# Feed-forward of a float32 decoder trunk in two phases, with hi and lo activations streamed as one operand

## Chip, cores, metric

The kernel runs on one NeuronCore of a Trainium2 chip, as one launch. The metric is the device time of the whole program in microseconds (us). Engines are named as in the profile: PE is TensorE (matmul), PEld its weight load, DVE VectorE, ACT ScalarE, POOL GpSimd, SP the queue that issues DMAs.

## What is computed

A trunk of 4 layers on 256 tokens of width 1024, all in float32. Every layer is a macaron: a feed-forward half, a token mixer (differential attention, RWKV-7, sliding-window attention, differential attention), a second feed-forward half. So there are 8 feed-forwards, each with its own weights (34.6 MB).

```python
D_MODEL, SEQ, DEPTH, D_FF = 1024, 256, 4, 2816
def swiglu(h, w_in, w_out):
    gate, up = jnp.split(h @ w_in, 2, axis=-1)
    return (jax.nn.silu(gate) * up) @ w_out
...
    for i in range(DEPTH):
        mod = (cond @ ada_w[i] + ada_b[i])[:, None, :]
        sh1, sc1, g1, sh2, sc2, g2, sh3, sc3, g3 = jnp.split(mod, N_MOD, axis=-1)
        h = modulate(rms_norm(x, norm_g[i, 0]), sh1, sc1)
        x = x + 0.5 * g1 * swiglu(h, ffn_w_in[i, 0], ffn_w_out[i, 0])
        h = modulate(rms_norm(x, norm_g[i, 1]), sh2, sc2)
        ...   # x = x + g2 * mixer(h)
        h = modulate(rms_norm(x, norm_g[i, 2]), sh3, sc3)
        x = x + 0.5 * g3 * swiglu(h, ffn_w_in[i, 1], ffn_w_out[i, 1])
```

## The kernel before

Activations are kept feature-major: a tile is 128 features on the partitions by 256 tokens. A float32 product is carried by float32r (one-pass) matmuls on operands split exactly as x = hi + lo. ACT makes hi (a cast, L266), DVE makes lo (raw minus hi, L268). For one 128x128 block of weights `mm3` (L282) issues three matmuls with 256 columns each: W_hi times a_hi (L284), W_hi times a_lo (L285), W_lo times a_hi (L286). Each has its own weight load, so W_hi is loaded twice. What follows calls such a block a **weight tile**, and one matmul a **pass**.

Weights come in units of 1 MB (128 x 2048 floats) by `load` (L257): SP fetches the unit into one of 4 `raw` buffers, then it is split in chunks of 512 columns into one of 4 `hi` and 4 `lo` buffers. The adaLN modulation vectors are made on DVE from 1 MB `ada` units (L341), spread over the kernel; a feed-forward takes 16 of them.

`ffn` (L596) loops over 11 pairs j of inner tiles (256 inner features). Per j: two units of W_in (gate, up), one unit of W_out of the pair before; 32 weight tiles for gate and up into two PSUM banks (gate of both inner tiles in one, up in the other), then `silu`, product and split of the inner activation `g` (ACT L675 and L678, DVE L676 and L679, each on 128x512), then 16 weight tiles that add the pair's part of the output into four PSUM banks, `acc`, which hold all 8 output tiles for the whole feed-forward. In the last pair `out_last` finishes two output tiles at a time and `residual` (L566) turns each into the new x (DVE L569). For each new x, `stat_add` squares it (ACT L436) and sums the squares (POOL L444, the last ones on PE, L459), and `pre` makes the unscaled split operand `xh` of the next sub-layer (ACT L481, DVE L482).

A sub-layer starts with `first_units` (L511): its first three units run on `xh` while the norm factor is still being computed; `make_h` (L487) then builds the scaled operand `h` (DVE L503 and L506, ACT L505), and `unraw` (L528) scales the banks made from `xh` (DVE L533).

PE, DVE, ACT, POOL and SP each work their own queue in order. A scheduler fixes the order of each queue when the program is built; buffers that are not yet free become waits.

Of the kernel before, what the change touches and what calls it, by code (L numbers as in the profile page):

```python
# [19 lines left out]
P = 128  # L20
# [4 lines left out]
PA, PB = 2, 9  # L25
DFF = 2816
NPAIR = DFF // 256
# [10 lines left out]
# modulation units taken in a feed-forward layer and in the three mixers  # L38
FF_ADA, MIX_ADA = 16, (8, 4, 4)
# [7 lines left out]
# ------------------------------------------------------------------ host layout  # L47
# [90 lines left out]
def _colunits(w):  # L138
    """[1024, n*256] -> [n, 128, 8*256]"""
# [4 lines left out]
def _rowunits(w):  # L144
    """[n*256, 1024] -> [n, 128, 2*1024]"""
# [4 lines left out]
def _layout(i):  # L150
# [33 lines left out]
    w = g["ffn_w_in"].reshape(DEPTH * 2, ND, P, 2, NPAIR, 256)  # L184
    o["ffi"] = np.ascontiguousarray(w.transpose(0, 4, 3, 2, 1, 5).reshape(DEPTH * 2 * NPAIR * 2, P, 2048))
    w = g["ffn_w_out"].reshape(DEPTH * 2 * NPAIR, 2, P, D)
    o["ffo"] = np.ascontiguousarray(w.transpose(0, 2, 1, 3).reshape(DEPTH * 2 * NPAIR, P, 2048))
# [37 lines left out]
# ------------------------------------------------------------------ device  # L225
class Trunk:
    def __init__(self, tc, ctx, aps, plan):
# [7 lines left out]
        self.sl = e(tc.tile_pool(name="sl", bufs=4))  # L235
        self.pp = e(tc.tile_pool(name="pp", bufs=2, space=bass.MemoryType.PSUM))
# [7 lines left out]
    def ps(self, tag):  # L244
        """One PSUM bank; the four tags have two banks each."""
        return self.pp.tile([P, 512], F32, tag="ps" + tag, name=self.n("ps" + tag))

    def slab(self, tag, shape=(P, 2048), dtype=F32):
        return self.sl.tile(list(shape), dtype, tag=tag, name=self.n(tag))

    # -------------------------------------------------- weights
# [5 lines left out]
    def load(self, src, cols=2048, raw=None, pool=False):  # L257
        """DMA a 1 MB unit and split it exactly: returns (hi, lo)."""
# [5 lines left out]
        for o in range(0, cols, self.chunk):  # L264
            sl = slice(o, min(o + self.chunk, cols))
# [5 lines left out]
    def ahead(self, aps, lead=4):  # L271
        """unit(u) -> (hi, lo) of aps[u]; units are loaded up to `lead` ahead of the one asked for."""
        todo, got = list(aps), []

        def unit(u):
            while todo and len(got) < u + lead:
                got.append(self.load(*todo.pop(0)))
            return got[u]

        return unit  # L280

# [6 lines left out]
    # -------------------------------------------------- constants, inputs  # L288
# [1147 lines left out]
```

## Time and profile before

| | |
|---|---|
| median of 3 runs | 2347.99 us (2346.6 to 2350.0) |
| span of the profiled execution (no other time of it is listed) | 2353.5 us |
| PE busy | 2220.3 us, 94% of the span, 17714 matmuls |
| DVE busy | 1752.3 us, 74% |
| ACT busy | 1193.5 us, 51% |
| POOL busy | 371.1 us, 16% |
| HBM read | 501.84 MB |

The page gives busy time by engine over the whole span. A matmul's listed duration contains its pipeline latency, and matmuls overlap; the time that one costs is the distance from its start to the start of the next. The granted clock of PE is listed as a share of full speed: 1.0 is 2.4 GHz, 0.5 is 1.2 GHz. The same caution holds for DVE, whose neighbours overlap by about 0.08 us.

### The profile page before, as it was taken

What the parts mean: (1) busy time and instruction counts of PE and PEld (TensorE: products, weight loads), DVE (VectorE), ACT (ScalarE), POOL (GpSimd) and SP (SyncE); (2) the same over time, 40 slices, a digit from 0 to 9 for tenths busy, and PEclk for the clock granted to TensorE, in tenths of its full rate; (3) what the DMA queues carried; (4) which work ended last, traced back from release to release, by engine and by line L of the source; (5) the groups of instructions that cost most, each with busy time, mean ns of one, the idle gap of its engine ahead of it and who ended that gap; (6) DMA issues with size and microseconds to landing.
All of it is one profiled execution on the core that took longest, in us unless ns stands there. A gap on an engine that the chain in (4) does not pass through costs nothing.

```text
span 2353.5 us, 44720 instructions
## 1 busy us (share of the span) xinstructions
PE 2220.3 (94%) x17714; PEld 2151.1 (91%) x17714; DVE 1752.3 (74%) x3437; ACT 1193.5 (51%) x2594; POOL 371.1 (16%) x1047
## 2 busy tenths in 40 slices
PE   3999889999999899998999999999999999889999
PEld 3999888999999778887999999989999999778999
DVE  6886877988875668876887885668888965777654
ACT  2544656544544455433644644487445544656542
POOL 4000454000100232221100100221001000444000
PEclk9999999999999999988999999999999999999999
DMA  7886454888675410005688695535987765463552
GB/s 284 339 330 223 146 198 179 307 337 322 238 270 191 164 55 19 19 19 182 242 341 314 231 354 180 188 126 185 359 316 285 288 233 180 146 214 126 204 190 73
DMA packets 72498, 505.78 MB, mean 215 GB/s; under 512 B 8032, under 2 KB 10592, under 8 KB 11744
## 3 DMA queue, kind: packets, MB, share of 16 engines
q1 hardware_dynamic: 70992, 501.68, 57.8%
q8 instruction: 139, 2.28, 0.4%
q10 hardware_dynamic: 1296, 1.25, 0.2%
q14 instruction: 71, 0.58, 0.1%
HBM read 501.84 MB, written 1.05 MB: 214 GB/s over the span
## 4 chain that ended last, share of the span: by engine, by line
PE 46%; DVE 8%; POOL 5%; issue 4%; ACT 2%; DMA 0%; DVEq 0%; POOLq 0%; ACTq 0%
PE psa L286 4%; PE psa L285 4%; PE psa L284 4%; PE psd L285 4%; PE psd L286 4%; PE psd L284 3%; PE psb L284 3%; PE psb L285 3%; PE psb L286 3%; PE psc L285 2%; PE psc L284 2%; PE psc L286 2%; DVE lo L268 2%; DVE xh L482 1%; DVE xr L503 1%
## 5 line engine op out<-in xcount | busy, mean ns | idle before, releaser
L266 ACT CAST hi<-raw 128x512 fp32r<-128x512 f32 x1314 | 739.2, 618 | 726.4 <-issue 633.0
L268 DVE TENSOR_TENSOR lo<-raw,hi 128x512 fp32r<-128x512 f32 x1306 | 841.2, 690 | 236.1 <-ACT hi L266 235.1
L284 PE MATMUL psa<-h,hi 128*128 128x256 f32 x1360 | 385.4, 284 | 20.4 <-ACT hi L266 8.1
L285 PE MATMUL psa<-h,hi 128*128 128x256 f32 x1360 | 386.2, 284 | 3.0 <-DVE h L506 3.0
L286 PE MATMUL psa<-h,lo 128*128 128x256 f32 x1360 | 385.6, 284 | 0.0
L285 PE MATMUL psd<-h,hi 128*128 128x256 f32 x1280 | 362.6, 283 | 2.9 <-DVE h L506 2.8
L286 PE MATMUL psd<-h,lo 128*128 128x256 f32 x1280 | 362.1, 283 | 0.5 <-POOL lo L268 0.5
L284 PE MATMUL psd<-h,hi 128*128 128x256 f32 x1280 | 360.7, 282 | 0.0
L341 DVE SCALAR_TENSOR_TENSOR ada<-ada,cb 128x1024 f32<-128x1024 f32 x232 | 276.2, 1224 | 18.3 <-DMA ada<-in_ada_dram 18.2
L284 PEld LDWEIGHTS psa<-h,hi 128*128 128x128 f32 x1360 | 260.9, 192 | 22.0 <-ACT hi L266 8.8
L285 PEld LDWEIGHTS psa<-h,hi 128*128 128x128 f32 x1360 | 259.1, 191 | 4.3 <-DVE h L506 4.1
L286 PEld LDWEIGHTS psa<-h,lo 128*128 128x128 f32 x1360 | 259.1, 191 | 0.0
L285 PEld LDWEIGHTS psd<-h,hi 128*128 128x128 f32 x1280 | 242.7, 190 | 5.3 <-DVE h L506 5.2
L284 PEld LDWEIGHTS psd<-h,hi 128*128 128x128 f32 x1280 | 244.1, 191 | 0.0
L286 PEld LDWEIGHTS psd<-h,lo 128*128 128x128 f32 x1280 | 242.3, 189 | 0.9 <-POOL lo L268 0.8
L286 PE MATMUL psb<-g,lo 128*128 128x256 f32 x704 | 199.3, 283 | 0.0
L284 PE MATMUL psb<-g,hi 128*128 128x256 f32 x704 | 199.3, 283 | 0.0
L285 PE MATMUL psb<-g,hi 128*128 128x256 f32 x704 | 199.2, 283 | 0.0
L285 PE MATMUL psc<-g,hi 128*128 128x256 f32 x704 | 199.0, 283 | 0.0
L286 PE MATMUL psc<-g,lo 128*128 128x256 f32 x704 | 199.0, 283 | 0.0
L284 PE MATMUL psc<-g,hi 128*128 128x256 f32 x704 | 198.9, 283 | 0.0
L484 POOL CAST xh<-shs 128x4 fp32r<-128x4 f32 x80 | 34.7, 441 | 1003.4 <-PE psa L286 528.0
(367 smaller groups left out, 4808.2 us busy)
## 6 DMA issues: line engine op xcount, KB each, us to landing
raw<-in_ffi_dram SPq DMA_DIRECT2D x183, 1024.0 KB, 5.2
ada<-in_ada_dram SPq DMA_DIRECT2D x116, 1024.0 KB, 7.4
raw<-in_ffo_dram SPq DMA_DIRECT2D x88, 1024.0 KB, 5.0
raw<-in_ada_dram SPq DMA_DIRECT2D x24, 1024.0 KB, 4.9
raw<-in_daqk_dram SPq DMA_DIRECT2D x16, 1024.0 KB, 4.9
raw<-in_rwr_dram SPq DMA_DIRECT2D x12, 1024.0 KB, 5.0
raw<-in_dav_dram SPq DMA_DIRECT2D x8, 1024.0 KB, 4.9
raw<-in_dao_dram SPq DMA_DIRECT2D x8, 1024.0 KB, 4.9
```

Source lines behind the costliest of these rows:

```text
L266: nc.scalar.copy(hi[:, sl], raw[:, sl])
L268: eng.tensor_tensor(lo[:, sl], raw[:, sl], hi[:, sl].bitcast(F32), op=ALU.subtract)
L284: nc.tensor.matmul(out, whi, ahi, start=start, stop=False, skip_group_check=True)
L285: nc.tensor.matmul(out, whi, alo, start=False, stop=False, skip_group_check=True)
L286: nc.tensor.matmul(out, wlo, ahi, start=False, stop=stop, skip_group_check=True)
L341: nc.vector.scalar_tensor_tensor(wk, wk, 1.0, self.cond, op0=ALU.mult, op1=ALU.mult, accum_out=raw[:, k:k + 1])
L482: nc.vector.scalar_tensor_tensor(h[:, 1, :T], self.x[d], a[:, d:d + 1], h[:, 0, :T].bitcast(F32), op0=ALU.mult, op1=ALU.subtract)
L484: nc.gpsimd.tensor_copy(h[:, :, T:], self.shs[:, :, d])
L503: nc.vector.scalar_tensor_tensor(t, self.x[d], ac, r, op0=ALU.mult, op1=ALU.mult)
```

## The change

Only `ffn` and the helpers below it change, and two buffer sizes.

- `mm2` takes the place of `mm3` inside the feed-forward, except in the three units that `first_units` runs (two in the very first feed-forward): W_hi times [a_hi | a_lo] as one matmul with 512 columns into the two halves of a PSUM bank, then W_lo times a_hi with 256 columns into the first half. So a weight tile takes two passes and two weight loads in place of three. The sum of the two halves is made when the bank is read: ACT copies the second half to SBUF, DVE adds the first half to it.
- The loop is turned into two phases. Phase 1 goes over 22 single inner tiles f; a unit of W_in now holds gate and up of one inner tile, and each takes a PSUM bank of its own. All 22 `g` tiles stay in SBUF. Phase 2 goes over the 8 output tiles d: 22 weight tiles accumulate in one bank, in two units of 0.72 MB. Then x(d) is formed at once: ACT scales the second half by the gate, POOL (DVE for d of 6 and 7) adds the old x, DVE adds the gated first half; `became` starts `stat_add` and `pre` of it.
- Units are split in chunks of 1024 columns (704 in phase 2); the first four keep 512. `hi` and `lo` have 3 buffers in place of 4. RWKV keeps its r and k in tiles of their own, and no longer in a `hi` and a `lo` buffer.
- The 16 `ada` units of a feed-forward are spread over f = 4 to 19 (10 of them) and d = 0 to 5 (6).

```diff
+    def mm2(self, bank, whi, wlo, a, start, stop):
+        nc.tensor.matmul(bank.rearrange("p (a t) -> p a t", a=2), whi, a, start=start, stop=False,
+                         skip_group_check=True)
+        nc.tensor.matmul(bank[:, :T], wlo, a[:, 0], start=False, stop=stop, skip_group_check=True)
...
-FF_ADA, MIX_ADA = 16, (8, 4, 4)
+FF_ADA, MIX_ADA = (10, 6), (8, 4, 4)
...
+        self.nslab = {"raw": 4, "hi": 3, "lo": 3}
...
+            for f in range(n0, NF):
...
+                w = unit(f)
+                if 4 <= f < 20:
+                    spread(0, 16)
+                tag = "adb"[f % 3]
+                bs = [self.ps(tag), self.ps(tag)]
+                self.project2(w, hs, bs)
+                gt, up = pair()
+                for b, t in zip(bs, (gt, up)):
+                    nc.scalar.copy(t, b[:, T:])
+                    nc.vector.tensor_tensor(t, b[:, :T], t, op=ALU.add)
+                nc.scalar.activation(gt, gt, AF.Silu)
+                finish(gt, up)
...
+            for d in range(ND):
+                bank = self.ps(("aaddbbcb" if rw else "aaddbbcc")[d])
+                for half in range(2):
+                    w = [t[:, :FO].rearrange("p (k c) -> p k c", c=P) for t in unit(NF + 2 * d + half)]
+                    if d < 6:
+                        spread(1, 12)
+                    for k in range(NF // 2):
+                        i = half * (NF // 2) + k
+                        self.mm2(bank, w[0][:, k], w[1][:, k], gs[i], start=(i == 0), stop=(i == NF - 1))
+                t = hp.tile([P, T], F32, tag="gt", bufs=3, name=self.n("hl"))
+                nc.scalar.activation(t, bank[:, T:], AF.Copy, scale=gate[:, d:d + 1])
+                (nc.gpsimd if d < 6 else nc.vector).tensor_tensor(t, t, self.x[d], op=ALU.add)
+                x = self.xp.tile([P, T], F32, tag="x", name=self.n("x"))
+                nc.vector.scalar_tensor_tensor(x, bank[:, :T], gate[:, d:d + 1], t, op0=ALU.mult, op1=ALU.add)
+                self.became(d, x)
...
-                    dst = self.slab(("hi", "lo")[i], (P, ND, T))
+                    dst = rp.tile([P, ND, T], F32, name=self.n("rk"))
```

Inside a feed-forward, PE's queue before, for a gate or up product (psa is the bank, h the activation, hi and lo the weights):

```order
L284 MATMUL psa_7344<-h_7003,hi_7295 128x256
L285 MATMUL psa_7344<-h_7003,hi_7295 128x256
L286 MATMUL psa_7344<-h_7003,lo_7296 128x256
L284 MATMUL psa_7344<-h_7008,hi_7295 128x256
L285 MATMUL psa_7344<-h_7008,hi_7295 128x256
L286 MATMUL psa_7344<-h_7008,lo_7296 128x256
```

and the same place now:

```order
L289 MATMUL psb_4937<-h_4295,hi_4812 128x512
L291 MATMUL psb_4937<-h_4295,lo_4813 128x256
L289 MATMUL psb_4937<-h_4300,hi_4812 128x512
L291 MATMUL psb_4937<-h_4300,lo_4813 128x256
L289 MATMUL psb_4937<-h_4305,hi_4812 128x512
```

Three passes of 256 columns have become one of 512 and one of 256; in all, PE's queue goes from 16148 to 12294 rows.

DVE's queue in the loop over inner tiles, before (gf and g are the product and the lo part of two inner tiles at once, lo the weights' split, the first rows wait for PE):

```order
L676 TENSOR_TENSOR gf_5791<-sil_5790,psa_5793 128x512 [waits PE_49]
L268 TENSOR_TENSOR lo_5969<-raw_5966,hi_5968 128x512 [waits DMAHW1_49,Activation_49]
L268 TENSOR_TENSOR lo_5969<-raw_5966,hi_5968 128x512 [waits Activation_49]
L679 TENSOR_TENSOR g_5789<-gf_5791,g_5789 128x512 [waits Activation_49]
L268 TENSOR_TENSOR lo_5969<-raw_5966,hi_5968 128x512 [waits Activation_49] x2
L341 SCALAR_TENSOR_TENSOR ada_6178,modr_6180<-ada_6178,cb 128x1024 [waits DMAHW5_49]
```

and now, for one inner tile (gt and up are its gate and up parts):

```order
L688 TENSOR_TENSOR gt_5133<-psb_5099,gt_5133 128x256 [waits PE_49]
L352 SCALAR_TENSOR_TENSOR ada_6680,modr_5968<-ada_6680,cb 128x1024 [waits DMAHW1_49]
L352 SCALAR_TENSOR_TENSOR ada_6680,modr_5968<-ada_6680,cb 128x1024
L688 TENSOR_TENSOR up_5134<-psb_5100,up_5134 128x256 [waits Activation_49]
L271 TENSOR_TENSOR lo_5147<-raw_5144,hi_5146 128x1024 [waits DMAHW6_49]
L653 TENSOR_TENSOR up_5134<-gt_5133,up_5134 128x256 [waits DVE_49]
L271 TENSOR_TENSOR lo_5147<-raw_5144,hi_5146 128x1024 [waits Activation_49]
L655 TENSOR_TENSOR g_5140<-up_5134,g_5140 128x256 [waits Activation_49]
```

Four short rows per inner tile (two adds, product, lo part) stand where two long ones per pair stood, and between them the split of a later unit in two rows.

## Rows read from the trace of the kernel before

**Rows 1.** The page, part 1: busy us (share of the span) and instructions.

```profile
PE 2220.3 (94%) x17714; PEld 2151.1 (91%) x17714; DVE 1752.3 (74%) x3437; ACT 1193.5 (51%) x2594; POOL 371.1 (16%) x1047
```

**Rows 2.** Busy time by stretch (us from the span's start; length, then PE, PEld, DVE, ACT, POOL busy with instruction counts, granted clock of PE, DMA share, GB/s): two stretches inside feed-forwards, and the first 40 us of one.

```profile
1150.00:1300.00 150.00, 150.00 (x1260) 149.92 (x1259) 129.38 (x225) 68.41 (x128) 2.19 (x2) 1.00 0.86 325
1345.00:1505.00 160.00, 159.73 (x1342) 159.73 (x1343) 111.33 (x189) 71.91 (x135) 0.61 (x3) 1.00 0.66 242
...
600.00:640.00 40.00, 39.42 (x328) 39.01 (x327) 39.43 (x78) 24.07 (x50) 0.00 (x0) 1.00 0.71 255
```

**Rows 3.** Timeline of PE inside a feed-forward, at full clock (start us, listed duration us).

```profile
499.95 0.28 PE L286 MATMUL psa<-h,lo 128*128 128x256 f32 x1
500.07 0.28 PE L284 MATMUL psa<-h,hi 128*128 128x256 f32 x1
500.18 0.28 PE L285 MATMUL psa<-h,hi 128*128 128x256 f32 x1
500.30 0.28 PE L286 MATMUL psa<-h,lo 128*128 128x256 f32 x1
```

**Rows 4.** Timeline of PE at the end of the RWKV mixer, where the clock is granted at half: the same passes.

```profile
1122.16 0.41 PE L286 MATMUL psb<-h,lo 128*128 128x256 f32 x1
1122.38 0.41 PE L284 MATMUL psb<-h,hi 128*128 128x256 f32 x1
1122.59 0.41 PE L285 MATMUL psb<-h,hi 128*128 128x256 f32 x1
```

**Rows 5.** Timeline of PE in RWKV at full clock: matmuls in true float32. Each is recorded as two (x2), each with its own weight load.

```profile
1002.90 0.59 PE L1353 MATMUL psd<-bon,con 128*128 128x256 f32 x2
1003.33 0.59 PE L1354 MATMUL psd<-lr,lw 128*128 128x256 f32 x2
1003.76 0.59 PE L1355 MATMUL psd<-lr,lw 128*128 128x256 f32 x2
```

**Rows 6.** Timeline of PE in RWKV at full clock: eight records of only 64 columns, each with a load of 128x128 weights, and the pass behind them.

```profile
890.64 1.00 PE L1271 MATMUL psc<-hi,zl 128*128 128x64 f32 x8
891.45 0.36 PE L284 MATMUL psd<-h,hi 128*128 128x256 f32 x1
```

**Rows 7.** Timeline of DVE (start us, listed duration us; x4 is four in a row): the pieces of which DVE's work is made.

```profile
604.09 0.42 DVE L533 TENSOR_TENSOR sil<-psa,rsq 128x256 f32<-128x256 f32 x1
604.43 0.42 DVE L533 TENSOR_TENSOR gf<-psd,rsq 128x256 f32<-128x256 f32 x1
...
606.88 1.28 DVE L268 TENSOR_TENSOR lo<-raw,hi 128x512 fp32r<-128x512 f32 x2
608.09 1.68 DVE L506 SCALAR_TENSOR_TENSOR h<-xr,mod,h 128x256 fp32r<-128x256 f32 x4
609.69 0.88 DVE L503 SCALAR_TENSOR_TENSOR xr<-x,mod,rsq 128x256 f32<-128x256 f32 x2
...
1212.21 1.22 DVE L341 SCALAR_TENSOR_TENSOR ada<-ada,cb 128x1024 f32<-128x1024 f32 x1
1213.35 0.09 DVE L341 DVE_READ_ACCUMULATOR ada<-ada,cb 128x1 f32 x1
```

**Rows 8.** Costliest groups of ACT (count, busy us, mean ns of one, idle before): weight cast, silu, cast of g, and a copy of 256 columns out of PSUM.

```profile
L266 ACT CAST hi<-raw 128x512 fp32r<-128x512 f32 x1314 | 739.2, 618 | 726.4 <-issue 633.0 <-PE psb L285 39.3 <-DMA raw<-in_ffi_dram 13.3
...
L675 ACT ACTIVATE sil<-psa 128x512 f32<-128x512 f32 x40 | 23.7, 592 | 10.9 <-PE psa L286 10.9
...
L541 ACT CAST o<-on 128x256 fp32r<-128x256 f32 x16 | 6.5, 405 | 26.9 <-DVE on L883 26.9
L1276 ACT COPY hi<-psc 128x256 f32<-128x256 f32 x16 | 6.0, 374 | 11.8 <-PE psc L1275 11.6
```

**Rows 9.** Who waited for whom (total us, times, longest): DVE's split of the weights, for ACT's cast.

```profile
DVE lo L268 <- ACT hi L266: 235.1, 170, 3.2
```

**Rows 10.** Busy time by stretch, columns as in rows 2: the three places where a feed-forward follows a feed-forward, each as a gap of PE and the stretch at half clock behind it.

```profile
588.80:590.90 2.10, 0.09 (x2) 0.04 (x1) 2.10 (x5) 1.00 (x3) 2.10 (x4) 1.00 0.00 0
591.10:594.60 3.50, 3.50 (x14) 3.09 (x13) 1.82 (x4) 1.25 (x4) 0.16 (x2) 0.51 0.00 0
1322.10:1324.20 2.10, 0.11 (x2) 0.01 (x1) 2.10 (x5) 1.01 (x4) 2.10 (x4) 1.00 0.06 27
1325.00:1328.40 3.40, 3.40 (x15) 3.03 (x14) 1.70 (x5) 0.73 (x2) 0.00 (x0) 0.50 0.01 2
1809.70:1811.80 2.10, 0.08 (x2) 0.02 (x1) 2.10 (x5) 1.01 (x4) 2.10 (x4) 1.00 0.00 0
1813.10:1816.50 3.40, 3.40 (x15) 3.13 (x14) 2.17 (x5) 0.59 (x2) 0.81 (x2) 0.50 0.00 0
```

**Rows 11.** Timeline of PE at the first of these gaps (what ended the idle time stands in brackets).

```profile
590.86 0.55 PE L459 MATMUL psc<-ssum,con 128*128 128x256 f32 x1 [2.01 <-POOL ssum L444]
```

**Rows 12.** Timeline of DVE at the same place: the last new x, and the norm factor made from the squares.

```profile
591.01 0.47 DVE L569 SCALAR_TENSOR_TENSOR x<-psb,mod,x 128x256 f32<-128x256 f32 x1
...
594.91 0.45 DVE L390 STREAM_TRANSPOSE rsqt<-psc 128x256 f32<-128x256 f32 x1 [1.99 <-PE psc L459]
...
599.99 0.45 DVE L422 STREAM_TRANSPOSE rsq<-ry 128x256 f32<-128x256 f32 x1 [2.91 <-POOL ry L416]
```

**Rows 13.** Busy time by stretch, columns as in rows 2: the first 40 us of the kernel, and a feed-forward.

```profile
0.00:40.00 40.00, 7.89 (x23) 5.73 (x24) 20.60 (x35) 10.21 (x21) 16.95 (x27) 1.00 0.95 374
1640.00:1790.00 150.00, 150.00 (x1264) 150.00 (x1263) 129.09 (x223) 67.55 (x127) 2.19 (x2) 1.00 0.87 330
```

More of the change, by code (lines that the diff above doesn't have):

```diff
@@ L24 @@
 DEPTH = 4
-PA, PB = 2, 9
 DFF = 2816
-NPAIR = DFF // 256
+NF = DFF // P
+FO = NF // 2 * P
 NEG = -1e30
@@ L248, in slab @@
     def slab(self, tag, shape=(P, 2048), dtype=F32):
-        return self.sl.tile(list(shape), dtype, tag=tag, name=self.n(tag))
+        return self.sl.tile(list(shape), dtype, tag=tag, bufs=self.nslab[tag], name=self.n(tag))
     def fetch(self, src, cols=2048):
@@ L255, in fetch, with load @@
         return raw
-    def load(self, src, cols=2048, raw=None, pool=False):
+    def load(self, src, cols=2048, raw=None, pool=False, chunk=None):
         nc = self.nc
@@ L263, in load @@
         lo = self.slab("lo", dtype=F32R)
-        for o in range(0, cols, self.chunk):
-            sl = slice(o, min(o + self.chunk, cols))
+        chunk = chunk or self.chunk
+        for o in range(0, cols, chunk):
+            sl = slice(o, min(o + chunk, cols))
             nc.scalar.copy(hi[:, sl], raw[:, sl])
@@ L570, in residual, with became @@
                                        op0=ALU.mult, op1=ALU.add)
+        self.became(d, t)
+    def became(self, d, t):
         self.x[d] = t
@@ L585, in project, with project2 @@
             self.mm3(out[f], hi[:, k, cs], lo[:, k, cs], hs[k][:, 0], hs[k][:, 1], start=(k == 0 and (own or f == 0)), stop=(k == ND - 1))
+    def project2(self, w, hs, banks):
+        hi = w[0].rearrange("p (k c) -> p k c", k=ND)
+        lo = w[1].rearrange("p (k c) -> p k c", k=ND)
+        for f, b in enumerate(banks):
+            for k in range(ND):
+                cs = slice(f * P, (f + 1) * P)
+                self.mm2(b, hi[:, k, cs], lo[:, k, cs], hs[k], start=(k == 0), stop=(k == ND - 1))
     def load_rest(self):
@@ L597, in ffn @@
         nc, A = self.nc, self.A
-        half = 0 if s == 0 else 1
-        base = (l * 2 + half) * NPAIR
+        n = l * 2 + (0 if s == 0 else 1)
         self.t1 = 4
@@ new lines, in ffn, with spread @@
+            src = []
+            for f in range(NF):
+                src.append((A["ffi"][n * NF + f], 2048, dict(raw=got[f] if f < len(got) else None, pool=start and f < 2,
+                                                             chunk=512 if f < 4 else 1024)))
+            src += [(A["ffo"][n * 2 * ND + i], FO, dict(chunk=FO // 2)) for i in range(2 * ND)]
+            unit = self.ahead(src, 3)
+            gs = []
+            pump = [0.0, 0.0]
+            def spread(part, m):
+                pump[part] += FF_ADA[part] / m
+                k = int(pump[part] + 1e-6)
+                pump[part] -= k
+                self.ada(k)
@@ new lines, in finish, with pair @@
+            def finish(gate, up):
+                g = hp.tile([P, 2, T], F32R, tag="g", bufs=NF, name=self.n("g"))
+                nc.vector.tensor_tensor(up, gate, up, op=ALU.mult)
+                nc.scalar.copy(g[:, 0], up)
+                nc.vector.tensor_tensor(g[:, 1], up, g[:, 0].bitcast(F32), op=ALU.subtract)
+                gs.append(g)
+            def pair():
+                return [hp.tile([P, T], F32, tag=t, bufs=3, name=self.n(t)) for t in ("gt", "up")]
+            n0 = 3 if self.xh else 2
@@ new lines, in ffn @@
+            unit(0)
+            banks, raw, hs = self.first_units([unit(f) for f in range(n0)], lambda: self.make_h(l, s, hp), "adb"[:n0])
+            for f in range(n0):
+                bg, bu = banks[2 * f], banks[2 * f + 1]
+                gt, up = pair()
+                if raw:
+                    cg = self.unraw(bg, gt)
+                    cu = self.unraw(bu, up)
+                    nc.scalar.activation(gt, gt, AF.Silu, bias=cg)
+                    nc.vector.tensor_scalar(up, up, cu, None, op0=ALU.add)
+                else:
+                    nc.scalar.activation(gt, bg[:, :T], AF.Silu)
+                    nc.vector.tensor_copy(up, bu[:, :T])
+                finish(gt, up)
@@ new lines, in ffn @@
+            for f in range(n0, NF):
+                if f == 10:
+                    self.load_rest()
+                w = unit(f)
[4 more added lines that the diff above has]
+                self.project2(w, hs, bs)
+                gt, up = pair()
+                for b, t in zip(bs, (gt, up)):
+                    nc.scalar.copy(t, b[:, T:])
+                    nc.vector.tensor_tensor(t, b[:, :T], t, op=ALU.add)
+                nc.scalar.activation(gt, gt, AF.Silu)
+                finish(gt, up)
@@ new lines, in ffn @@
+            gate = self.mod(l, 3 * s + 2)
+            rw = self.nxt is not None and self.nxt[1] == 1 and self.nxt[0] % 3 == 1
+            for d in range(ND):
[13 more added lines that the diff above has]
+                self.became(d, x)
@@ L1396, in run @@
         self.acc_p, self.chunk = 0.0, 512
-        self.rate = {(l, s): (MIX_ADA[l % 3] if s == 1 else FF_ADA) for l in range(DEPTH) for s in range(3)}
+        self.rate = {(l, 1): MIX_ADA[l % 3] for l in range(DEPTH)}
         self.setup()
```

100 lines of the change are left out of this document (11 added, 89 removed).

## Prediction

> **What bounds the kernel now.** I read the page's busy shares first: PE is busy 94% of the span, DVE 74%, ACT 51% [rows 1]. A share over the whole span doesn't say what a stage waits for, so the stretches come next. Inside the feed-forwards PE is busy 150.00 of 150 us and 159.73 of 160 us, at full clock, with DVE at 129 and 111 us [rows 2]. There PE is the bound and nothing else is; only in the first 40 us of a feed-forward is DVE as full as PE (39.43 against 39.42 us) [rows 2].
>
> So the question is what one pass costs PE. The listed 0.28 us is latency. The starts stand 0.12 us apart [rows 3], and the count gives it closer: 1260 passes in 150.00 us are 119 ns each, 1342 in 159.73 us are 119 too [rows 2]. A weight tile of three passes is 357 ns. A stream of 256 columns at 2.4 GHz is 106.7 ns, so 12 ns of each pass are something else. Two rows say what kind of thing. At half clock the same passes start 0.21 us apart [rows 4], which is 256 columns at 1.2 GHz (213 ns) with nothing added: the extra vanishes when the stream gets longer. And eight records of only 64 columns, which stream in 27 ns, still take 0.81 us together [rows 6], 0.10 us each: something of about 0.1 us per pass, the load of 128x128 weights being the one thing that they share with the others, goes on beside the stream and sets the pace when the stream is short. At 107 ns of stream the two are nearly equal, and the pass takes a little more than either.
>
> **What the change does to a pass.** No row shows a pass of 512 columns in float32r. The nearest is the true float32 matmul of 256 columns: three of them start 0.43 us apart, each is two records with a weight load each [rows 5], so 0.215 us per record. That is 512 columns at 2.4 GHz (213 ns) plus 2 ns, with the load hidden. I take 216 ns for the new 512-column pass. The 256-column pass behind it must still cover the load of the next W_hi, so I leave it at 119. New weight tile: 216 + 119 = 335 ns, 22 ns less than 357.
> The bounds: if the extra 12 ns belong to each pass whatever its length, the tile is 225 + 119 = 344 ns, 13 ns less. If the 256-column pass gets its load hidden too, it falls to 107 + 2 = 109 and the tile is 325 ns, 32 less. I take 335 because the float32 records are passes of just that length with just that load.
> How many: a feed-forward has 528 weight tiles (352 in, 176 out), eight have 4224. The three units of `first_units` keep three passes (48 tiles in seven feed-forwards, 32 in the first): 368. So 3856 tiles change: 3856 x 22 ns = **85 us** off PE's path (bounds 50 and 123).
>
> Weighed against a rule. The 256-column passes take 119 ns and the 512-column records 215 ns [rows 2, 5], so per column the long one is cheaper by a tenth. The Trainium skill, page TensorE: Matmul & The Clock Gate, section Back-to-back issue gap, gives a warm gap of N/2.4 + 2.5 ns for a single matmul of N columns. By it, as an estimate, the tile would go from 328 to 325 ns, and the change would save 10 us, not 85. The trace agrees with it for the 512-column records and not for the 256-column passes; it is a rival below.
>
> **The ends of the feed-forwards.** Before, the last two pairs finish all eight x in a burst; the POOL sums of squares come late, PE waits 2.01 us for them [rows 11] and then runs some 3.4 us at half clock, which costs half of that. The three places where a feed-forward follows a feed-forward all show it [rows 10]: 3 x (2.0 + 1.7) = **11 us**. After, an output tile takes 22 x 335 ns = 7.4 us, so x(0) to x(6) are long squared and summed when the last one comes. What is late next: x(7) goes through ACT, DVE twice, ACT, each about 0.4 us [rows 7, 8], some 2 us; PE has 36 passes on `xh` (4.3 us) before it needs its square. So the gap goes, and I count the 11 us. The gaps before and inside the mixers stay.
>
> **What is added, and where it lies.** The evacuation. Per inner tile DVE now does two adds and a product and a lo part, 256 columns each: 4 x 0.335 us (604.09 to 604.43 in [rows 7]). The split is 2 chunks of 1024; a 512 one takes 0.605 (two in 606.88 to 608.09), one operation on 1024 columns 1.14 (1212.21 to 1213.35) [rows 7]: 2.28 us. 10/16 of an `ada` unit at 2 x 1.14: 1.43 us. Together 1.34 + 2.28 + 1.43 = 5.05 us of DVE per inner tile, against 16 x 335 ns = 5.36 us of PE. So PE hides it, but only just: DVE is 94% full in phase 1, where a pair before took 12 x 0.605 + 2 x 0.605 + 2 units of `ada` 4.6 = 13.0 us of DVE in 48 x 357 ns = 17.1 of PE. If that cover went, every inner tile would cost what DVE takes beyond 5.36 us, in 153 tiles (20 in the first feed-forward, 19 in the others).
> ACT per inner tile: four half-chunks at most 0.62 each, two copies out of PSUM 0.37, silu at most 0.59, cast 0.41 [rows 8]: 4.2 us at most, hidden.
> Phase 2, per output tile: DVE 4 chunks of 704 (between 0.605 and 1.14, by their length 0.80), one `ada` unit 2.28, x and `xh` 0.4 each (four in 608.09 to 609.69) [rows 7]: 6.3 us against 7.4 of PE. DMA: 1.44 + 1.05 MB in 7.4 us are 336 GB/s; the kernel's first stretch shows 374, and a feed-forward has run at 330 with PE full [rows 13]. Hidden, with little room.
>
> **Waits that can come.** (1) Inner tile 3 is the first that needs the scaled `h` and a bank made free by `unraw`. The norm factor takes from 594.91 to 600.4 [rows 12], 5.5 us after the squares are in; add 4.3 us before and the eight `h` at 2 x 0.4 us each [rows 7], with two `unraw` and a split between them: about 19 to 20 us after the end of the feed-forward before, while PE comes there after 144 passes at 119 ns and three sums at 0.43 us, 18.4 us, and then needs one `h` per 335 ns. I count 1 us in seven feed-forwards, **7 us** (0 to 21). (2) With 3 `hi` buffers ACT's cast of a unit waits until PE has left the third unit before it, and what is queued behind the cast on ACT (in a mixer the exponentials and copies of the heads) waits with it. The unit itself is needed two units later, 11 us in a mixer, so PE is not starved; for ACT's queue I count 5 us over the mixers (0 to 20; no row shows it, and a better order could be worth a few us the other way). (3) The last x passes ACT and one more DVE step: 1 us.
>
> **Sum.** 85 + 11 - 7 - 5 - 1 = 83 us. The profiled span is 2353.5, so 2270 us in a profile; the timed runs lie 5.5 us lower, 2347.99 - 83 = **2265 us**. With its small terms at their bounds this case runs from 2245 to 2290.
>
> **Rivals.**
> A fixed 12 ns per pass (tile 344): for it, the passes are the same 119 ns with DVE at 86% and at 70% [rows 2], so nothing that comes and goes makes them long; against it [rows 4, 5]. 2348 - 50 - 11 + 13 = 2300 us.
> The short pass gains as well (tile 325): for it, W_lo's load is over long before its pass starts. 2348 - 123 - 11 + 13 = 2227 us.
> DVE becomes the bound in phase 1. For it: 94% leaves 0.31 us per inner tile, DVE's rows form a chain with ACT (copy, add, silu, product, cast, lo), and DVE has waited 170 times for ACT's cast, 235.1 us in all, 1.4 us each [rows 9]. Against it: two units of lookahead and six banks, so a wait costs only where DVE can't catch up. Its price is (idle per tile - 0.31) x 153: from 0.85 us of idle (83/153 + 0.31) the whole gain is lost and the kernel is slower; at one full wait of 1.4 us per tile it is 2265 + 167 = 2432 us, at half a wait 2265 + 60 = 2325.
> The passes saved are worth almost nothing: only the 2 ns over the bare stream [rows 5] go with each, 3856 x 2 = 8 us, and the rest of the 119 ns goes with the columns. Against it, the half-clock passes show no cost per column beyond the clock [rows 4]. 2348 - 8 - 11 + 13 = 2342 us, and 2350 with nothing. (It is what the Trainium skill's gap rule, cited above from TensorE: Matmul & The Clock Gate, would make of the change.)
>
> **Chances.** Forecast 0.56; fixed cost 0.13; short pass too 0.10; DVE-bound but still faster 0.09, DVE-bound and slower 0.06; almost nothing 0.06 (half of it within the bound of no change, some of it slower). About 0.2% (5 us) is what a measurement of this kernel can tell from no change. So faster 0.88, same 0.05, slower 0.07. The range takes in the tile at 325 and at 344 with their waits and the milder half of the DVE case: 2220 to 2325.
>
> **What would show it.** In the profile after: starts in phase 2 in the rhythm 216, 119; a different rhythm sets the first term. PE busy near 100% from inner tile 6 on, with no PE waits on `lo` or on a bank; if they are there, DVE is the bound and its busy time in phase 1 is whole. No gap behind L470's sums and full clock where a feed-forward follows one. PE waiting for `h` at inner tile 3 by about 1 us. In the mixers PE's idle as before, save some us on ACT's casts. The prediction is wrong if the 512-column pass takes over 225 ns, or if PE stands still in phase 1 by over 0.3 us per inner tile.

## The result, and the profile after

The changed kernel takes **2372.61 us** (median of 4 runs, 2371.44 to 2377.18) against 2348.99 us of the kernel before in the same session (2346.6 to 2350.21): ratio 1.0103, 95% interval 1.0089 to 1.0117. It is 1% slower where 3.5% faster (2265 us) was forecast. The profiled spans are 2370.2 and 2353.5 us.

The page, part 1, of the kernel after (answers to [rows 1]):

```profile
PE 2200.3 (93%) x13858; PEld 1961.9 (83%) x13858; DVE 1847.3 (78%) x3538; ACT 1302.6 (55%) x2713; POOL 422.4 (18%) x1095
```

PE has 3856 matmuls less, as announced, but only 20 us less work. To see where the time went, both traces are cut at one event that both have: the start of the last matmul that sums the squares of x (L459 or L452 before, L470 or L463 after), which opens every sub-layer. The time from one to the next, in us (the last feed-forward to PE's last matmul):

| | before | after | difference |
|---|---|---|---|
| eight feed-forwards | 1565.4 | 1556.2 | -9.2 |
| two differential attentions | 154.2 + 156.8 | 170.2 + 170.5 | +29.7 |
| RWKV, sliding window | 349.5 + 101.2 | 345.8 + 100.2 | -4.7 |

The feed-forwards gain 9 us in place of 88 (the forecast's 83 without the 5 us that it took off for the mixers), and two mixers whose code the change doesn't touch lose 30. First the feed-forwards. Timeline of PE after (start us, listed duration us): phase 2, phase 1, and phase 1 at half clock (answers to [rows 3, 4]):

```profile
560.18 0.39 PE L289 MATMUL psd<-g,hi 128*128 128x512 f32 x1
560.41 0.28 PE L291 MATMUL psd<-g,lo 128*128 128x256 f32 x1
560.53 0.39 PE L289 MATMUL psd<-g,hi 128*128 128x512 f32 x1
...
460.18 0.40 PE L289 MATMUL psb<-h,hi 128*128 128x512 f32 x1
460.42 0.28 PE L291 MATMUL psb<-h,lo 128*128 128x256 f32 x1
460.54 0.39 PE L289 MATMUL psb<-h,hi 128*128 128x512 f32 x1
...
430.76 0.63 PE L289 MATMUL psa<-h,hi 128*128 128x512 f32 x1
431.19 0.41 PE L291 MATMUL psa<-h,lo 128*128 128x256 f32 x1
431.40 0.63 PE L289 MATMUL psa<-h,hi 128*128 128x512 f32 x1
```

The rhythm is 230, 117 ns in phase 2 (in the second feed-forward 174 of 176 long passes at 230), and not 216, 119. Over all weight tiles at full clock, from the start of one L289 to the next into the same bank and without the stops of PE, the mean is 347.8 ns in phase 2 and 351.8 in phase 1; the same count before gives 359.4 for the tiles of W_out and 356.0 for those of W_in. So the saving is 11.6 ns x 1408 tiles + 4.2 ns x 2448 = 27 us. At half clock the same two passes take 427 and 213 ns, which is 512 and 256 columns at 1.2 GHz with nothing added.

Busy time by stretch after (columns as in [rows 2]), phase 1 and phase 2 of the second feed-forward:

```profile
440.00:530.00 90.00, 90.00 (x516) 78.85 (x515) 85.52 (x149) 54.08 (x97) 1.02 (x1) 1.00 0.84 301
545.00:590.00 45.00, 45.00 (x262) 39.67 (x261) 40.61 (x61) 23.01 (x41) 16.33 (x17) 1.00 0.88 316
```

PE is full, with DVE at 95 and 90%: the DVE rival did not come. PE does stand still where a feed-forward begins behind a mixer, in three places of four. Timeline of PE at inner tile 3 of these three feed-forwards (idle time and what ended it in brackets), then DVE in front of the first of these places, and at the same place before:

```profile
428.70 0.77 PE L289 MATMUL psa<-h,hi 128*128 128x512 f32 x1 [5.56 <-DVE gt L544]
...
1164.26 0.77 PE L289 MATMUL psa<-h,hi 128*128 128x512 f32 x1 [5.65 <-DVE gt L544]
...
1647.21 0.77 PE L289 MATMUL psa<-h,hi 128*128 128x512 f32 x1 [4.81 <-ACT h L516]
```

```profile
416.36 0.45 DVE L433 STREAM_TRANSPOSE rsq<-ry 128x256 f32<-128x256 f32 x1 [2.91 <-POOL ry L427]
...
416.78 1.22 DVE L352 SCALAR_TENSOR_TENSOR ada<-ada,cb 128x1024 f32<-128x1024 f32 x1
...
417.92 2.49 DVE L271 TENSOR_TENSOR lo<-raw,hi 128x512 fp32r<-128x512 f32 x4
420.33 1.27 DVE L514 SCALAR_TENSOR_TENSOR xr<-x,mod,rsq 128x256 f32<-128x256 f32 x3
421.51 2.36 DVE L271 TENSOR_TENSOR lo<-raw,hi 128x1024 fp32r<-128x1024 f32 x2
...
428.14 0.42 DVE L544 TENSOR_TENSOR gt<-psa,rsq 128x256 f32<-128x256 f32 x1
```

```profile
404.80 0.45 DVE L422 STREAM_TRANSPOSE rsq<-ry 128x256 f32<-128x256 f32 x1 [2.64 <-POOL ry L416]
...
408.90 0.42 DVE L533 TENSOR_TENSOR sil<-psa,rsq 128x256 f32<-128x256 f32 x1
```

The norm factor is there at 416.8. Then come a modulation unit and the splits of two weight units, 6 us of them between the factor and most of the h; and `unraw`, which frees bank a for inner tile 3, comes behind all but two of the h steps: 11.3 us after the factor, where it came 3.7 us after it before (405.2 to 408.9). The clock falls to half during each of these three gaps, and behind them PE's passes run 4.0, 5.9 and 4.3 us at half clock.

Where a feed-forward follows a feed-forward, two of the three gaps of [rows 10] are gone; one, of 2.84 us, stays. Timeline of DVE and PE there, and of PE at the end of the feed-forward in front of RWKV:

```profile
602.23 1.23 DVE L352 SCALAR_TENSOR_TENSOR ada<-ada,cb 128x1024 f32<-128x1024 f32 x1 [4.23 <-DMA ada<-in_ada_dram]
...
605.46 0.48 DVE L706 SCALAR_TENSOR_TENSOR x<-psc,mod,hl 128x256 f32<-128x256 f32 x1
...
606.50 0.81 PE L470 MATMUL psc<-sq,con 128*128 128x256 f32 x2 [2.84 <-ACT sq L447]
...
798.91 1.22 PE L463 MATMUL psc<-sq,con 128*128 128x256 f32 x2 [3.14 <-ACT sq L447]
```

At the first of the two places, a modulation unit that had not landed yet stood in DVE's queue in front of the last x, and DVE waited 4.23 us for its DMA. In front of RWKV, where no passes on `xh` cover the time, PE waits 3.14 us for the square of the last x, and 0.72 us before (for the sum on POOL).

The mixers, by stretch: the two differential attentions before, after, and in the first run below (columns as in [rows 2]).

```profile
244.60:398.90 154.30, 135.31 (x977) 126.80 (x976) 115.49 (x278) 95.70 (x251) 71.92 (x226) 0.96 0.49 174
2007.20:2164.00 156.80, 136.91 (x976) 128.17 (x975) 115.67 (x279) 95.56 (x251) 68.35 (x225) 0.95 0.46 162
```

```profile
239.50:409.70 170.20, 141.63 (x975) 132.72 (x975) 134.40 (x315) 94.84 (x250) 76.88 (x226) 0.90 0.58 204
2011.20:2181.60 170.40, 139.55 (x976) 131.01 (x975) 113.33 (x274) 94.92 (x250) 63.49 (x225) 0.91 0.41 142
```

```profile
239.40:396.80 157.40, 137.03 (x975) 128.43 (x974) 114.70 (x278) 94.47 (x248) 69.29 (x226) 0.95 0.50 173
1996.10:2150.90 154.80, 135.97 (x976) 127.45 (x975) 112.72 (x276) 94.83 (x248) 65.95 (x225) 0.94 0.47 163
```

The matmuls are the same in number. After, PE stands some 10 us longer in each, and its granted clock falls from 0.96 to 0.90, so the same matmuls take 3 to 6 us more as well. In the first one DVE has 37 rows more (36 of modulation units drawn forward), in the second none, and they lose 16 and 14 us: it is not DVE's work. (In a_mix_lo below neither has any, and both stay slow.)

### The profile page after: what moved, and what is told of

The parts are those of the page before. It is cut to its first block, busy times and chain, and to the rows that moved or that the text cites. A ratio compares the mean times of both kernels' runs of the same rounds, so it can differ in the third digit from the quotient of the medians.

```text
span 2370.2 us, 37894 instructions
## 1 busy us (share of the span) xinstructions
PE 2200.3 (93%) x13858; PEld 1961.9 (83%) x13858; DVE 1847.3 (78%) x3538; ACT 1302.6 (55%) x2713; POOL 422.4 (18%) x1095
## 5 line engine op out<-in xcount | busy, mean ns | idle before, releaser
L271 DVE TENSOR_TENSOR lo<-raw,hi 128x512 fp32r<-128x512 f32 (+2 forms) x894 | 803.4, 923 | 198.9 <-ACT hi L269 196.3
L269 ACT CAST hi<-raw 128x512 fp32r<-128x512 f32 (+2 forms) x902 | 692.5, 801 | 314.3 <-issue 93.9
L289 PE MATMUL psa<-h,hi 128*128 128x512 f32 x896 | 326.7, 403 | 19.9 <-DVE gt L544 11.8
L289 PE MATMUL psb<-h,hi 128*128 128x512 f32 x784 | 277.7, 395 | 0.0
L289 PE MATMUL psd<-h,hi 128*128 128x512 f32 x768 | 272.2, 395 | 0.0
L289 PEld LDWEIGHTS psa<-h,hi 128*128 128x128 f32 x896 | 173.0, 193 | 64.8 <-issue 13.0
L291 PE MATMUL psb<-h,lo 128*128 128x256 f32 x784 | 220.4, 281 | 0.8 <-DVE lo L271 0.8
L289 PEld LDWEIGHTS psb<-h,hi 128*128 128x128 f32 x784 | 148.5, 189 | 34.4
L289 PEld LDWEIGHTS psd<-h,hi 128*128 128x128 f32 x768 | 145.5, 189 | 34.2
L291 PEld LDWEIGHTS psb<-h,lo 128*128 128x128 f32 x784 | 147.8, 188 | 1.2 <-DVE lo L271 1.2
L289 PE MATMUL psb<-g,hi 128*128 128x512 f32 x374 | 131.1, 394 | 0.0
L289 PE MATMUL psa<-g,hi 128*128 128x512 f32 x352 | 122.7, 392 | 0.0
L289 PE MATMUL psd<-g,hi 128*128 128x512 f32 x352 | 122.7, 392 | 0.0
L289 PE MATMUL psc<-g,hi 128*128 128x512 f32 x330 | 115.2, 392 | 0.0
```

Of the source, the lines that this page charges most:

```text
L269: nc.scalar.copy(hi[:, sl], raw[:, sl])
L271: eng.tensor_tensor(lo[:, sl], raw[:, sl], hi[:, sl].bitcast(F32), op=ALU.subtract)
L289: nc.tensor.matmul(bank.rearrange("p (a t) -> p a t", a=2), whi, a, start=start, stop=False, skip_group_check=True)
L291: nc.tensor.matmul(bank[:, :T], wlo, a[:, 0], start=False, stop=stop, skip_group_check=True)
```

## Experiments

**1. A fourth hi and lo buffer in the differential attentions (a_mix4).**

```diff
     def slab(self, tag, shape=(P, 2048), dtype=F32):
+        if self.xsl is not None and tag in self.xn:
+            self.xn[tag] += 1
+            if self.xn[tag] % 4 == 0:
+                return self.xsl.tile(list(shape), dtype, tag="x" + tag, bufs=1, name=self.n(tag))
...
     def diff(self, l):
+            self.xsl = c.enter_context(self.tc.tile_pool(name=self.n("xs"), bufs=1))
```

> The changed kernel, with a fourth hi and a fourth lo buffer inside the two differential attentions only (taken from the room that the feed-forward's inner tiles need elsewhere). From the squares' last sum of one sub-layer to that of the next, the two differential attentions take 154.2 and 156.8 us before the change, 170.2 and 170.5 us after it: 29.7 us of the loss. If the third buffer is the cause (theory 1), they fall back to about 154 and 157 us, and the kernel to about 2372.6 - 30 = 2343 us. If the loss comes from the order of the heads, from the modulation units that moved or from the clock (rival), they stay at 170 us and the kernel at 2370 or more.

Measured: 2339.02 us, ratio to before 0.9957 (0.9942 to 0.9973). The two attentions take 157.4 and 154.8 us (rows above): 28.5 of the 29.7 us are back, and the kernel is now 0.4% faster than the one before. It was expected at 2343 us.

**2. Three buffers in the kernel before (b_hilo3).**

```diff
+        self.nslab = {"raw": 4, "hi": 3, "lo": 3}
...
-                    dst = self.slab(("hi", "lo")[i], (P, ND, T))
+                    dst = rp.tile([P, ND, T], F32, name=self.n("rk"))
```

> The kernel before, with 3 hi and 3 lo buffers in place of 4 (RWKV's r and k in tiles of their own, as in the changed kernel) and nothing else. Theory 1 (the buffers cost the differential attentions 30 us, the feed-forwards nothing): 2349 + 30 = 2379 us, the two differential attentions at about 170 us each, the eight feed-forwards at 1565 us together as before. Rival (the buffers are innocent): 2349 us, the differential attentions at 154 and 157 us. If the feed-forwards need the fourth buffer too, they show it as waits of PE on lo, and the kernel is slower still.

Measured: 2432.45 us, ratio 1.0352 (1.0333 to 1.0372). The attentions take 171.0 and 172.7 us, as theory 1 says. The eight feed-forwards take 1612.5, 47 us more, so theory 1 was wrong on them, and the time is 53 us above its 2379. So the old feed-forward needed the fourth buffer too. The new one gains 6 us when its first units have a fourth (run 7); with four buffers throughout it was not run.

**3. One of the two buffers at a time (a_mix_hi, a_mix_lo).** As 1, but the rule in `slab` holds for hi alone or for lo alone.

> The changed kernel with a fourth hi buffer in the differential attentions and still three lo buffers. With both, the two took 157 and 155 us in place of 170. If what hurts is the cast at the head of ACT's queue, waiting for PE to leave a hi buffer while the heads' exponentials and copies stand behind it (the forecast's reason), this alone brings back most of it: 2372 - 25 = about 2347 us. If DVE's subtraction then waits for the lo buffer in the same way, with the heads' DVE work behind it (rival), this brings back little: 2365 us or more.

> The changed kernel with a fourth lo buffer in the differential attentions and still three hi buffers. If the cast on ACT is what hurts, nothing comes back: 2372 us. If DVE's wait for lo is what hurts, most comes back: 2347 us. If each of the two queues is stopped by its own missing buffer, both of these runs stay near 2370.

Measured: 2362.92 us (ratio 1.0045, 1.0029 to 1.0061) and 2375.38 us (1.0096, 1.0079 to 1.0114). The attentions take 163.9 and 166.2 us with hi, 171.5 and 171.3 with lo. A hi buffer alone brings back 10.6 us, a lo buffer alone nothing, both 28.5: neither the forecast's reason (ACT alone) nor its rival holds by itself. Who waited for whom in the first attention (total us, times, longest), the cast before and after, and DVE's subtraction in a_mix_hi:

```profile
ACT hi L266 <- PE psb L285: 9.9, 5, 5.2
ACT hi L269 <- PE psb L297: 6.3, 4, 2.7
ACT hi L269 <- PE psb L296: 5.3, 4, 3.4
DVE lo L276 <- PE psb L302: 2.6, 3, 1.8
```

With a fourth hi alone, DVE's subtraction waits for PE to leave a lo buffer (in both attentions 8 times, 8.4 us); before, after, in a_mix4 and in a_mix_lo it never does there. That fits two stops one behind the other: the cast first, and once it is free, the subtraction. But the cast's own waits for PE hardly differ, 21.0 us in the two attentions before and 18.1 after, so that they don't show how 30 us come of it.

**4. The merged pass taken apart (a_three).**

```diff
-        nc.tensor.matmul(bank.rearrange("p (a t) -> p a t", a=2), whi, a, start=start, stop=False,
-                         skip_group_check=True)
+        nc.tensor.matmul(bank[:, :T], whi, a[:, 0], start=start, stop=False, skip_group_check=True)
+        nc.tensor.matmul(bank[:, T:], whi, a[:, 1], start=False, stop=False, skip_group_check=True)
```

> The changed kernel with the 512-column pass taken apart again: W_hi times a_hi into the first half of the bank and W_hi times a_lo into the second, as two passes of 256 columns; phases, buffers and evacuation stay. If merging two passes is worth what the two traces show (theory: a weight tile of 357 ns against 346.7 in phase 2 and 352.7 in phase 1), this kernel is 1408 x 10 + 2448 x 4 ns = 24 us slower than the changed one, about 2397 us, with PE's starts 119 ns apart. If the 7 ns come from elsewhere in the new structure (rival: three short passes there cost 350 ns too), it stays at 2372 us. If the forecast of 22 ns per tile was right and something else ate it, it is 85 us slower, 2457 us.

Measured: 2405.03 us (2397 expected), ratio 1.0237 (1.0215 to 1.0259), 32 us above the changed kernel; weight tiles of 359.9 ns in phase 2 and 356.4 in phase 1, the feed-forwards 26.4 us longer. The merge is worth what the two traces show, not 85 us, and the evacuation, the phases and the layout add half a nanosecond to a tile at most (359.4 and 356.0 before).

**5. What a pass costs (pass_probe, pass_probe2).** In phase 2, each weight tile but the first of an output tile:

```diff
+        c = (0, 512, 384, 256, 128, 512, 512, 64)[n]
...
+        for i, w in enumerate(ws):
+            self.nc.tensor.matmul(bank[:, :c], w, a[:, :c], start=False, stop=stop and i == 1, skip_group_check=True)
```

> The changed kernel with other passes in phase 2 of seven feed-forwards, so that it computes something else there: each weight tile but the first of an output tile issues two passes of 512 columns (second feed-forward), 384 (third), 256 (fourth), 128 (fifth), 512 with the same weights W_hi in both (sixth), 512 in bfloat16 (seventh), 64 (eighth); the first is as in the changed kernel. What is read is the distance from start to start, not the time of the whole. If a float32r pass costs a fixed 12 ns beside its stream, the starts stand 225, 172, 119 ns apart at 512, 384, 256 columns. If it costs a share of its columns (230 and 117 ns seen at 512 and 256), they stand 230, 173, 117 apart. If the load of the weights is the floor, 128 and 64 columns both take about 0.1 us. If the rest of the stream's cost is the 4 bytes of an element, bfloat16 takes 216 ns where float32r takes 230; if it is the new weights for each pass, the sixth feed-forward is no different only when equal weights are loaded again.

Timeline of PE in the first probe: 512, 384, 256, 128 columns, bfloat16 with 512, 64 columns at half clock.

```profile
579.63 0.39 PE L303 MATMUL psb<-g,hi 128*128 128x512 f32 x1
579.85 0.39 PE L303 MATMUL psb<-g,lo 128*128 128x512 f32 x1
...
785.01 0.33 PE L303 MATMUL psb<-g,hi 128*128 128x384 f32 x1
785.19 0.33 PE L303 MATMUL psb<-g,lo 128*128 128x384 f32 x1
...
1326.85 0.29 PE L303 MATMUL psc<-g,hi 128*128 128x256 f32 x1
1326.97 0.28 PE L303 MATMUL psc<-g,lo 128*128 128x256 f32 x1
...
1500.87 0.28 PE L303 MATMUL psc<-g,lo 128*128 128x128 f32 x1
1500.98 0.28 PE L303 MATMUL psc<-g,hi 128*128 128x128 f32 x1
...
2019.72 0.39 PE L303 MATMUL psc<-g,lo 128*128 128x512 bf16 x1
2019.95 0.39 PE L303 MATMUL psc<-g,hi 128*128 128x512 bf16 x1
...
2341.01 0.40 PE L303 MATMUL psa<-g,lo 128*128 128x64 f32 x1
2341.22 0.40 PE L303 MATMUL psa<-g,hi 128*128 128x64 f32 x1
```

Medians over some 325 starts each: 227 ns at 512 columns, 173 at 384, 120 at 256, 111 at 128; 227 with the same weights loaded again, 226 in bfloat16. From 256 to 512 columns that is the stream at 2.4 GHz (213.3, 160, 106.7) plus 13.7, 13, 13.3 ns: **a fixed 13 ns per pass** here, whatever its length, and for bfloat16 at 512 columns too. At 128 columns the floor is 111 ns; with 64 it is 112 at full clock (41 starts) and 213 at half.

> The changed kernel with other passes in phase 2, so that it computes something else there, and other places of h in phase 1. Phase 2, all but the first weight tile of an output tile: two passes of 512 columns with only 64 weight columns (second feed-forward), with only 64 rows (third), in true float32 with 512 columns (fifth) and with 256 (sixth), two of 256 columns that begin one column later (seventh), 512 with the two passes in two different banks (eighth); the first and fourth as in the changed kernel. A pass was 13 to 14 ns longer than its stream at 512, 384 and 256 columns. If that comes from reading and writing the same bank again, the eighth shows 216 in place of 227; if from the exchange of 128 weight columns or rows, the second or third shows less; if from nothing of this kind, all stay at 227. True float32 with 256 columns should repeat 0.43 us per matmul. Phase 1: h's lo part stands 258, 256, 264, 260 columns behind its hi part in the first four, and 256 with the whole shifted by 16, 1, 2, 8 columns in the others: if the place of the operand matters, the starts differ between these feed-forwards by some ns.

Timeline of PE in the second probe: true float32 with 512 and with 256 columns (two records, x2, per matmul), and the two banks in turn.

```profile
1600.34 1.02 PE L298 MATMUL psd<-g,hi 128*128 128x512 f32 x2
1601.20 1.02 PE L298 MATMUL psd<-g,lo 128*128 128x512 f32 x2
...
2100.29 0.59 PE L298 MATMUL psb<-g,hi 128*128 128x256 f32 x2
2100.72 0.60 PE L298 MATMUL psb<-g,lo 128*128 128x256 f32 x2
...
2660.10 0.40 PE L298 MATMUL psc<-g,hi 128*128 128x512 f32 x1
2660.33 0.40 PE L298 MATMUL psd<-g,lo 128*128 128x512 f32 x1
```

Medians: 227 ns with two banks, 230 with 64 weight columns, 227 with 64 rows; true float32 429 and 216 ns per record, which is two streams plus 2.5 ns. So neither the bank nor the size of the weights makes the 13 ns, and true float32 records don't have them. What does is open. Passes of 256 columns that begin one column later take 122 ns. Of the moved h, too, only the shift by one column stands out: median 236 ns for the long pass, 231 to 233 in the other seven.

**6. h side by side (a_hflat, on top of 1).** `make_h` takes `t[:, :2 * T]` of a tile of 528 columns in place of `[P, 2, T + 2]`.

> The run with four buffers in the differential attentions, and besides the scaled h's hi and lo columns stored side by side (512 columns in a row, in tiles of 2112 bytes per partition) in place of two rows of 258 in 2064 bytes. In phase 1 a weight tile takes 352.7 ns, in phase 2, where g lies in a row, 346.7. If the place of the operand is what costs the 6 ns (theory), the 2448 weight tiles of phase 1 gain 2448 x 6 ns = 15 us: 2324 us, with starts 230 and 117 ns apart. If the 6 ns come from what DVE, ACT and the DMAs do at the same time (rival), it stays at 2339 us and the starts at 233 and 120.

Measured: 2334.99 us, ratio 0.9919 (0.9903 to 0.9936); the profiled span is 3.0 us shorter than in 1. A tile of phase 1 goes from 351.7 to 350.1 ns: 4 us, not 15. The ratio moved further than the trace explains. Why phase 1 stays 3 ns per tile above phase 2 is open. The rival, what the other engines and the DMAs do at the time, does not fit: once PE runs without stops, the tiles' lengths repeat within 2 ns, every 8, 16 or 24 tiles (one, two or three rounds of the eight h) in the eight feed-forwards after the change, and every 8 in all of them here.

**7. The start of a feed-forward (a_ff4, a_c4, a_best, a_best_flat, all on top of 1).**

```diff
+            early = ExitStack()
+            self.xsl = early.enter_context(self.tc.tile_pool(name=self.n("xs"), bufs=1))
...
+                if f == 8:
+                    self.xsl = None
+                if f == 14:
+                    early.close()
+                    gp, ng = c.enter_context(self.tc.tile_pool(name=self.n("g2"), bufs=1)), NF - 14
...
-                tag = "adb"[f % 3]
+                tag = "adbc"[f % 4]
```

The first part is a_ff4, the last two lines are a_c4. In a_best and a_best_flat, which have both, the count of buffers also starts anew with each feed-forward.

> The run with four buffers in the differential attentions, and besides a fourth hi and a fourth lo buffer for the first units of each feed-forward (units issued before inner tile 8), in the room of the g tiles of inner tiles 14 to 21, which are not written yet then. Theory: behind a mixer PE stands 4.0, 5.7, 4.8 and 1.3 us at inner tile 3, because with three buffers the split of unit 3 can't start before PE has left unit 0 and so falls on DVE between the norm factor and the scaled h; after three of these gaps PE runs 3.4 to 6.8 us at half clock. With the fourth buffer the split is done earlier, the gaps fall below 1 us each and the kernel gains 2339 - 16 to 20 = about 2321 us. Rival: DVE has too much to do there in any order (its splits, modulation and h), the gaps stay and the time is 2339 us; or the closing of the early buffers stalls the split at inner tile 14, which would show as a PE gap there and a slower kernel.

> The run with four buffers in the differential attentions, and besides inner tiles from 3 on take the PSUM banks in the order c, a, d, b in place of a, d, b. Inner tile 3 then needs no bank that unraw has to make free. If the bank is what holds PE there (the row names DVE's gt out of psa at the gap of 5.7 us behind RWKV, ACT's h at the others), that gap goes and the kernel gains 4 to 8 us, to about 2333 us. If h, late behind the split, is what counts everywhere, the gaps stay at 4 to 6 us and the time at 2339 us.

> Both together: four buffers in the differential attentions, a fourth pair of buffers for the first units of each feed-forward (now counted so that unit 3 is the one that gets it, and not unit 0 or 1, which had to wait for the end of the feed-forward before), and the banks in the order c, a, d, b. If h behind the split and the bank behind unraw are the two causes, no mixer is followed by a gap of over 1.5 us at inner tile 3, half clock goes there, the gap of 5.1 us that stayed behind the sliding-window attention goes, and the kernel takes 2335 - 8 to 14 = about 2324 us, 0.988 of before. If DVE is simply too full there, it stays at 2335 us.

> The same, with the scaled h's hi and lo columns side by side. By the run that did this alone (FFNs 2 us shorter in the trace), 0 to 4 us less than the run without: 2320 to 2324 us. If the place of h in SBUF matters, phase 1 shows starts of 230 and 117 ns and 10 us or more are gained; if not, nothing.

| | time | ratio to before | feed-forwards in the trace |
|---|---|---|---|
| a_mix4 | 2339.02 | 0.9957 (0.9942 to 0.9973) | 1550.3 |
| a_ff4 | 2335.25 | 0.9924 (0.9909 to 0.9939) | 1544.4 |
| a_c4 | 2332.47 | 0.9914 (0.9900 to 0.9928) | 1539.9 |
| a_best | 2331.98 | 0.9913 (0.9898 to 0.9929) | 1545.2 |
| a_best_flat | 2325.64 | 0.9885 (0.9871 to 0.9900) | 1536.7 |

Timeline of PE at inner tile 3 behind RWKV and behind the sliding window, with the other bank (a_c4):

```profile
1142.79 0.51 PE L294 MATMUL psc<-h,hi 128*128 128x512 f32 x1 [1.27 <-DVE h L522]
...
1622.51 0.50 PE L294 MATMUL psc<-h,hi 128*128 128x512 f32 x1 [0.86 <-DVE h L522]
```

The bank alone takes the gaps from 5.7 and 4.8 us to 1.3 (and one of 1.0 behind it) and 0.9, also where the row had named h, and behind RWKV with DVE's rows in the same order as after the change: it was the bank that held PE. The early buffers alone mend RWKV's gap as well (1.2 us; `unraw` comes 3.7 us behind the factor there, and 11.3 after the change) and leave the sliding window's (5.1 us, ended by unraw's gt). a_c4 came out as expected (2333 us), a_ff4 14 us above its 2321. Together they gain nothing over the bank alone; my 2324 us for both was 8 too low. The last run, with h side by side, takes 6 us less than a_best (0 to 4 expected) and is 1.15% faster than the kernel before.

## Why the prediction was wrong

The time came out above the range, and slower in place of faster. No single term turns the sign: with the measured saving of a tile alone the sum is still 25 us on the faster side, with the measured mixers as well it is 0, and with inner tile 3 it is 16 us on the slower side.

- **What a pass costs** (85 us; measured 27). The step that failed is the choice of the true float32 record as the nearest row for the 512-column pass. Its 215 ns are right and come again in the probe (216), but they belong to float32 records: a float32r or bfloat16 pass of that length takes 226 to 233. What led there was reading [rows 4], half clock without any extra, as "the extra vanishes when the stream gets longer". It is gone at half clock whatever the length (427 and 213 ns for 512 and 256 columns), and at full clock it stays whatever the length, 13 ns at 512 columns as at 256. The sign of being wrong that the prediction named, a pass of over 225 ns, is what came. The rival of a fixed 12 ns had the right mechanism (225 + 119 = 344 forecast, 347 measured in phase 2), but its sum has a gain of 50 us; phase 1 gives only 4 ns per tile, which no case had and no run explains. The Trainium skill, page TensorE: Matmul & The Clock Gate, section Back-to-back issue gap, gives N/2.4 + 2.5 ns for a single matmul of N columns at full clock; here only the float32 records agree (216), the float32r passes stand at 227, 173 and 120 ns. By it, as an estimate, 10 us were to be gained. By the fixed cost it was 50; the measured 27 lie between.
- **Three buffers in the mixers** (5 us, bounds 0 to 20; measured 30). It said that "no row shows it" and took a bound of 20 by feeling; but [rows 8] have 39.3 us in which the cast waited for PE, with four buffers. It should have been found from what stands behind a stopped cast. Of the reason given, ACT's queue, the runs show a part: hi alone brings back 10.6 of 28.5 us. DVE's queue, stopped by lo, was left out. That the buffers are the cause is shown, by taking them away before and giving them back after. That the stops reach PE through the heads' chains is argued; no single wait in the trace carries the 30 us.
- **Inner tile 3** (7 us, bounds 0 to 21; measured 16.0 us of idle in three feed-forwards, and 14.2 us at half clock, which costs half of that: 23). The place and both reasons, h and the bank, were named. The bank was taken as one of two; in truth `unraw` stands behind the h in DVE's queue, and with another bank the gaps are nearly gone (run 7). A modulation unit and two whole units to split stood in front, where one split was counted. The clock that a stop of 5 us costs was not counted, although the same reasoning counted it for the ends.
- **The ends** (11 us): two of three gaps went, 7 us. The last x was counted at 2 us through ACT and DVE; where the gap stayed, a modulation unit in front of it waited for its DMA. In front of RWKV the last x costs 2.4 us more than before, where 1 us was counted for it.
- **DVE in phase 1**: right; 94% forecast, 95% measured, and PE is full all the same.

The sum by measured terms: -27 - 7 + 30 + 23 + 2 (the last x in front of RWKV) - 5 (RWKV and window, not forecast) is +16, against +16 us between the two traces from the first squares on. (The forecast's own sum for its small terms was a little off: with (1) and (2) at their bounds the case runs from 2253 to 2294, not from 2245 to 2290. Nothing hangs on it.)

## What to carry to other kernels

Before a cost is borrowed from another row, ask in which ways the rows differ (type of pass, clock), and measure the one that is left: a pass here has a fixed 13 ns at full clock, and merging two into one saved 12 ns in phase 2, and no share of the columns (in phase 1 only 4). A buffer taken from a shared ring is paid by every stage that uses the ring, also those that the diff doesn't show, so price it there or give it back there. In a queue that is worked in order, look at what frees the bank that PE needs next: taking a fourth bank into the turn was worth 10 us in the feed-forwards (1550.3 to 1539.9).

## What the runs showed of the hardware

- In phase 2 and the probes, at full clock, a one-pass float32r matmul starts N/2.4 + 13 ns after the one before, for 256 to 512 columns (227, 173, 120 ns). At 512 columns it is the same in bfloat16, with equal weights, 64 rows or two banks (226, 227, 227, 227), and 230 with 64 weight columns. In phase 1 it is 119 and 233 ns for 256 and 512. At half clock it is N/1.2 with nothing added (427, 213). True float32 records have 2.5 ns (429, 216).
- With 128 or 64 columns the floor is 111 or 112 ns at full clock; with 64 columns it is 213 ns at half clock, as long as 256 columns take there.
- The long pass changes by a few ns in fixed patterns. In phase 1 they go with the round of the h. In phase 2 they don't go with the operand: the third feed-forward's long passes start 230 ns apart in the first five output tiles and, on the same g, 232, 241, 235 ns in turn from the sixth on, where the float32 matmuls that sum the squares first stand in between; the eighth runs in that pattern throughout, the six others at 230. What sets it is open.
